# Half of the query tiles as fp16 pairs, top-k set up inside its generator, and 64 instead of 72 expert columns in the first stash

## The chip, the core and the metric

The kernel runs on one core of one Trainium2 chip. The metric is the device time of one execution in microseconds. The kernel before was measured three times: 982.04, 983.15 and 983.37 us, median 983.15 us. One execution was also profiled; its own time was 982.88 us, of which the profile's span (first to last instruction) is 980.8 us.

## What is computed

One decoder block on 256 tokens of width 1024: an attention mixer (nothing of it is touched here), and behind it a product-key expert layer (PEER), then a final RMSNorm. Of the expert layer, cut to what matters:

```python
def peer_ffn(h, wq, sub_keys, u, v):            # 16384 experts = 128 x 128, 8 heads, top 16
    ...
    q = (xc @ wq).reshape(PEER_CHUNK, PEER_HEADS, 2, PEER_QDIM // 2)   # 16 query tiles of 128
    sub = jnp.einsum('thpd,pkd->thpk', q, sub_keys)
    sv, si = lax.top_k(sub, PEER_TOPK)                                 # per head and half
    cand = sv[:, :, 0, :, None] + sv[:, :, 1, None, :]
    ...
    best, pos = lax.top_k(cand, PEER_TOPK)
    g = jax.nn.softmax(best, axis=-1)
    act = jax.nn.gelu(jnp.einsum('td,thkd->thk', xc, u[eid]))
    return jnp.einsum('thk,thkd->td', g * act, v[eid])
```

## The kernel before, in words

The kernel gathers no experts. It computes all 16384 activations as 128 columns j of 128 experts each (NJ = 128) and multiplies them by a gate matrix that is zero outside the chosen experts. Its stages behind the attention mixer are these.

**Inputs (u stage).** `u_step(j)` (L826) loads 512 KB of `peer_u` (`raw`, 5 buffers), splits the tile into two fp16 halves, and multiplies with the token matrix h, which is itself held as an fp16 pair `h16`: 8 blocks of the inner dimension times 3 products, 24 matmuls of 256 columns by `mm3` (L88). The split is `split16` (L800): ScalarE writes the high half (L805), VectorE the remainder with a checksum into `chk` (L806). The halves go to `w_hi` for even and `w_lo` for odd j, 3 buffers each. A GELU on ScalarE (L846) then writes column j of a stash, fp32, one slice of 256 tokens for each j. The stash has two tiles: `st0` with HJ = 72 columns and `st1` with the other 56; `st1` takes the memory of the top-k tiles and exists only once these are closed.

**Top-k beside it.** `topk_gen` (L868) is a generator whose pieces are pumped between the u steps (L1054). For each of 8 heads: two query tiles (`wq`, L872), two sets of sub-key scores with a top 16 on VectorE (`sub_scores`, L881), and a top 16 of 80 candidate sums. Query tiles 0 to 3 (heads 0 and 1) are made earlier; the other 12 are made here, each as 8 matmuls in fp32 over `wraw` (3 buffers) and the fp32 copy `h2`, which the profile lists as 16 instructions (L877). Then two groups of 14 pieces turn the winners into one-hot keys `kT` and gates `gT`. The pump schedule is none or one piece a step to j = 11, then 2, 2, 1 in turn to j = 29, then one a step; the 64 pieces end at j = 58.

**Gates.** `g_all(half)` (L1008) goes over 32 blocks of 8 tokens. `g_build` (L975) makes one-hot matrices A (128 columns) and B, Bl (as many columns as the stash half) on VectorE; `g_apply` (L994) makes 16 matmuls with that many columns each (L1000), and VectorE multiplies the result into the stash (L1004). Half 0 is paced over the u steps j = 62 to 123, 65 pieces. Columns j of the first stash that come after gating has begun (62 to 71) go another way: GELU into a tile `act` and a multiplication by the gates already there (L842 to L844).

**Outputs (v stage).** `v_step(j)` (L1091) loads 512 KB of `peer_v`, splits it in the same way, splits the stash column into `wt` (3 buffers, L1071 and L1076) and makes 12 matmuls of 512 columns (L1089). Half 1 of the gates is paced over the first HJ - 6 = 66 of these steps. From j = HJ on, `tail_prep` (L1118) loads 8 tiles of `ada_w` into the same `raw` buffers, one a step, and reduces them on VectorE (L1121). Small inputs of the tail are loaded by POOL's queue into `st0`, whose columns are free by then: `scratch(i)` (L1104) is its i-th stretch of four columns. `xc`, 1 MB, goes to stretches 16 and 17 (L1113).

**Repeated half.** Sums of the residues (`chk`) and of the first high halves (`big`) are tested at the end (`all_fit`, L1163). Only if one is out of range does a second program part (L1205) repeat the expert layer in another format; in these runs it is jumped over.

**Order.** The framework orders the instructions of each engine before the run, by priority (the place in the program) among those that its own model finds ready. `tc.high_priority(offset=None)` (L809, L873) puts loads and splits to the front of that order. At run time each engine works strictly in that order.

Of the kernel before, what the change touches and what calls it, by code (L numbers as in the profile page):

```python
# [13 lines left out]
F32 = mybir.dt.float32  # L14
# [43 lines left out]
def block_kernel(ctx: ExitStack, tc: tile.TileContext, I, out):  # L58
# [48 lines left out]

    SU, SH, SW, SV = 2.0 ** 13, 2.0 ** 8, 2.0 ** -3, 2.0 ** 9
    hchk = keep.tile([P, KD], F32, name="hchk")
    big = keep.tile([P, 3 + KD], F32, name="big")  # L110


    ph1 = ExitStack()
# [652 lines left out]
    for k in range(KD):  # L766
        t = nrm[:, k % 2]
        V.tensor_mul(t, x2g[:, k, 0:T], rstd2)
        S.activation(h2[:, k], t, AF.Identity, bias=mod[:, 24 + k:25 + k])
        S.activation(h16[0][:, k], t, AF.Identity, bias=shs[:, k:k + 1], scale=SH, accum_out=big[:, 3 + k:4 + k])  # L770
        V.scalar_tensor_tensor(h16[1][:, k], h2[:, k], SH, h16[0][:, k], ALU.mult, ALU.subtract,
                               accum_out=hchk[:, k:k + 1])
    qe = h2_pool.tile([P, 4, T], F32, name="qe")
# [6 lines left out]

    GS = 2.0 ** 15
    NJ = 128
    HJ = 72
    st0_pool = ctx.enter_context(tc.tile_pool(name="stash0", bufs=1))
    st = [st0_pool.tile([P, HJ, T], F32, name="st0")]
    NCHK = 3 * NJ + KD
    LOW = 2.0 ** 17
    LIM = 2.0 ** 16

# [2 lines left out]
    gT = keep2.tile([P, 2, T, 2], F16, name="gT")  # L792
    iota = keep2.tile([P, P], F16, name="iota")
    chk = keep2.tile([P, NCHK], F32, name="chk")
    G.memset(chk[:, 0:3 * NJ], 0.0)
    G.tensor_copy(chk[:, 3 * NJ:], hchk)
    first_one = {}
    bad_flag = keep2.tile([1, 1], I32, name="bad_flag")

    def split16(src, hi, lo, scale, i):  # L800
        kw = {}
        if i < 2 * NJ and i // NJ not in first_one:
            first_one[i // NJ] = i
            kw = dict(accum_out=big[:, 1 + i // NJ:2 + i // NJ])
        S.activation(hi, src, AF.Copy, scale=scale, **kw)  # L805
        V.scalar_tensor_tensor(lo, src, scale, hi, ALU.mult, ALU.subtract, accum_out=chk[:, i:i + 1])  # L806

    def load_split16(src, scale, i):
        with tc.high_priority(offset=None):  # L809
            t = load(src)  # L810
            hl = hl_pool.tile([P, D], F32R, name=("w_hi", "w_lo")[i % 2]).bitcast(F16)
            split16(t, hl[:, 0:D], hl[:, D:2 * D], scale, i)
        return hl[:, 0:D], hl[:, D:2 * D]
# [1 line left out]
    pg = ctx.enter_context(tc.tile_pool(name="pg", bufs=2, space=PSUM, reuse_waits="tile"))  # L815
    ps_u = ExitStack()
    pu = ps_u.enter_context(tc.tile_pool(name="pu", bufs=3, space=PSUM, reuse_waits="tile"))
    tk_stack = ExitStack()
    tk = tk_stack.enter_context(tc.tile_pool(name="tk", bufs=2, reuse_waits="tile"))
    tk1 = tk_stack.enter_context(tc.tile_pool(name="tk1", bufs=1, reuse_waits="tile"))  # L820

    act_box, hr_box = [], []
    done_j = [0]
    gated = [0]
# [20 lines left out]
        if n < T:  # L845
            S.activation(w[:, n:T], ps[:, n:T], AF.Gelu_apprx_tanh, scale=scale)  # L846

    iota_i = tk1.tile([P, P], I32, name="iota_i")
    G.iota(iota_i, pattern=[[1, P]], base=0, channel_multiplier=0)
    G.tensor_copy(iota, iota_i)  # L850
    c15 = tk1.tile([P, PH * TK], U32, name="c15")
    G.memset(c15, 15)
    sk = tk1.tile([P, 2, P], F32, name="sk")
    nc.scalar.dma_start(sk, I["peer_sub_keys"])
    nc.scalar.dma_start(h2d, h2)
    sv = tk1.tile([P, 2, 2, PH, TK], F32, name="sv")
    si = tk1.tile([P, 2, 2, PH, TK], U32, name="si")
    best = tk1.tile([P, 2, PH, TK], F32, name="best")
    bpos = tk1.tile([P, 2, PH, TK], U32, name="bpos")

    def top16(vals, tmp, vout, iout):
        V.max(vout[:, 0:8], vals)
        V.max_index(iout[:, 0:8], vout[:, 0:8], vals)
# [1 line left out]
        V.max(vout[:, 8:16], tmp)  # L865
        V.max_index(iout[:, 8:16], vout[:, 8:16], tmp)

    def topk_gen():  # L868
        for h in range(PH):
            qs = {p: qe[:, 2 * h + p] for p in range(2)} if h < 2 else {}  # L870

            def wq(p):  # L872
                with tc.high_priority(offset=None):  # L873
                    w = load(I["peer_wq"][2 * h + p], pool=tk, name="wraw", bufs=3)
                ps = pu.tile([P, T], F32, name="up")
                for k in range(KD):
                    PE.matmul(ps, w[:, k * P:(k + 1) * P], h2[:, k], start=k == 0, stop=k == KD - 1)  # L877
                qs[p] = tk.tile([P, T], F32, name="qT")
                S.copy(qs[p], ps)

            def sub_scores(p):  # L881
                sps = pg.tile([P, NT, P], F32, name="gps").rearrange("p a b -> p (a b)")[:, 0:256]
# [9 lines left out]
            for f, p in ((wq, 0), (wq, 1), (sub_scores, 0), (sub_scores, 1))[2 if h < 2 else 0:]:  # L892
# [144 lines left out]
    tg = topk_gen()  # L1037
    alive = True
    gg = None
    for j in range(NJ):  # L1040
        if not alive and gg is None:
            tk_stack.close()
            st1_pool = ctx.enter_context(tc.tile_pool(name="stash1", bufs=1))
            st.append(st1_pool.tile([P, NJ - HJ, T], F32, name="st1"))
            act_stack = ExitStack()
            act_box.append(act_stack.enter_context(tc.tile_pool(name="actp", bufs=2)))
            h2_stack.close()
            gp_stack = ExitStack()
            gp_box.append(gp_stack.enter_context(tc.tile_pool(name="gp", bufs=2, side="right", reuse_waits="tile")))
            gg, first = g_all(0), j + 3  # L1050
        u_step(j, True)
        done_j[0] = j + 1
        if alive:
            alive = pump(tg, j % 2 if j < 12 else (2, 2, 1)[j % 3] if j < 30 else 1)  # L1054
        elif j >= first:
            paced(gg, j - first, NJ - 4 - first)
    ps_u.close()
    act_stack.close()
    w_pool = ctx.enter_context(tc.tile_pool(name="wp", bufs=LAST))

    def outputs(half, gg):

        inner = ExitStack()
        py = inner.enter_context(tc.tile_pool(name="py", bufs=1, space=PSUM))
        if not half:
            wl_pool = inner.enter_context(tc.tile_pool(name="wl", bufs=LAST, side="right"))
# [43 lines left out]
        fg = scratch(1)  # L1110
        nc.gpsimd.dma_start(fg, I["final_g"].partition_broadcast(P))
        xf = [scratch(4), scratch(5)]
        xc = scratch(16, 2).rearrange("p (k t) -> p k t", k=KD)  # L1113
        nc.gpsimd.dma_start(xc, x2d)

        ada_b2 = scratch(15)[:, 0:48]
# [46 lines left out]
        def all_fit():  # L1163

            ok = scratch(2)[:, 0:NCHK]
            V.tensor_mul(ok, chk, chk)
            V.tensor_scalar(ok, ok, LIM * LIM, None, ALU.is_lt)
            V.tensor_mul(big[:, 1:], big[:, 1:], big[:, 1:])
            V.tensor_reduce(big[:, 0:1], ok, axis=AX.X, op=ALU.min)
            V.tensor_scalar_mul(big[:, 0:1], big[:, 0:1], LOW / (P - 0.5))  # L1170
            ps = pg.tile([P, NT, P], F32, name="gps").rearrange("p a b -> p (a b)")[0:1, 0:3 + KD]
            PE.matmul(ps, ones[:, 0:1], big, start=True, stop=True)
            small = scratch(2)[0:1, 0:3 + KD]
# [27 lines left out]

    outputs(True, g_all(1))
    gp_stack.close()
    rv = nc.values_load(bad_flag, min_val=0, max_val=1)
    with tc.If(rv > 0):  # L1205

        again = ExitStack()
        pu = again.enter_context(tc.tile_pool(name="pu", bufs=2, space=PSUM))
        gated[0] = 0
# [14 lines left out]
                pass  # L1224
        again.close()
        outputs(False, None)


def bucket_onehot():
# [67 lines left out]
```

## Time and profile before

| | us |
|---|---|
| median of 3 runs (982.04 to 983.37) | 983.15 |
| profiled execution, its own time | 982.88 |
| its span | 980.8 |
| TensorE (PE) busy in the span | 934.2 (95%) |
| VectorE (DVE) busy | 766.8 (78%) |
| ScalarE (ACT) busy | 494.2 (50%) |

How to read it: PE is TensorE's matmuls, PEld its weight loads, which overlap them; POOL is GpSimd, SP the engine that issues most DMAs. Matmuls are pipelined, each is listed longer (0.27 us for 256 columns) than the distance between two starts (0.11 us), so the distance of starts is what a matmul costs in a row of them. VectorE's rows overlap their successor by about 0.08 us in the same way. L12 is line 12 of the kernel before.

### The profile page before, as it was taken

What the parts mean: (1) busy time and instruction counts of PE and PEld (TensorE: products, weight loads), DVE (VectorE), ACT (ScalarE), POOL (GpSimd) and SP (SyncE); (2) the same over time, 40 slices, a digit from 0 to 9 for tenths busy, and PEclk for the clock granted to TensorE, in tenths of its full rate; (3) what the DMA queues carried; (4) which work ended last, traced back from release to release, by engine and by line L of the source; (5) the groups of instructions that cost most, each with busy time, mean ns of one, the idle gap of its engine ahead of it and who ended that gap; (6) DMA issues with size and microseconds to landing.
All of it is one profiled execution on the core that took longest, in us unless ns stands there. A gap on an engine that the chain in (4) does not pass through costs nothing.

```text
span 980.8 us, 18690 instructions
## 1 busy us (share of the span) xinstructions
PE 934.2 (95%) x7120; PEld 686.2 (70%) x7120; DVE 766.8 (78%) x2033; ACT 494.2 (50%) x899; POOL 17.9 (2%) x32
## 2 busy tenths in 40 slices
PE   5698997989999999999999999999999999999995
PEld 3697776979888888889999999544444443454442
DVE  6597879778657599658888888799999998656564
ACT  4246876475323365544444444544544554555542
POOL 0100010000000000000000000000000000000001
PEclk9899899899999999999999999999999999999998
DMA  8997646677554345765555555665555669756631
GB/s 285 319 329 252 218 130 211 224 252 263 174 193 151 108 166 179 248 203 177 190 175 191 175 187 179 204 205 193 184 189 188 214 208 332 235 178 207 199 124 48
DMA packets 54709, 198.26 MB, mean 202 GB/s; under 512 B 6269, under 2 KB 6605, under 8 KB 54226
## 3 DMA queue, kind: packets, MB, share of 16 engines
q1 hardware_dynamic: 52642, 189.90, 58.0%
q0 software_dynamic: 1248, 5.33, 2.1%
q10 hardware_dynamic: 720, 1.74, 0.5%
q8 instruction: 58, 0.95, 0.4%
q14 instruction: 41, 0.34, 0.1%
HBM read 193.22 MB, written 3.74 MB: 201 GB/s over the span
## 4 chain that ended last, share of the span: by engine, by line
PE 81%; DVE 7%; DMA 6%; ACT 3%; issue 2%; SPq 0%; DVEq 0%; ACTq 0%
PE y L1089 28%; PE up L89 11%; PE up L91 11%; PE up L90 11%; PE up L877 4%; PE gps L1000 3%; DMA raw<-in_ada_w_dram 3%; DMA adaw<-in_ada_w_dram 2%; PE mm L90 1%; PE mm L91 1%; PE mm L89 1%; PE lg L362 1%; PE o L536 1%; DVE w_lo L74 1%; PE gps L885 1%
## 5 line engine op out<-in xcount | busy, mean ns | idle before, releaser
L1089 PEld LDWEIGHTS <-wt 128*128 128x128 f16 x1500 | 143.9, 98 | 170.2 <-DVE wt L806 4.7
L805 ACT ACTIVATE w_lo<-raw 128x1024 f16<-128x1024 f32 x128 | 135.3, 1057 | 173.9 <-PE y L1089 83.3
L805 ACT ACTIVATE w_hi<-raw 128x1024 f16<-128x1024 f32 x128 | 135.2, 1056 | 170.5 <-PE up L91 85.4
L806 DVE SCALAR_TENSOR_TENSOR w_lo<-raw,w_lo 128x1024 f16<-128x1024 f32 x128 | 156.5, 1222 | 62.9 <-ACT w_lo L805 60.5
L806 DVE SCALAR_TENSOR_TENSOR w_hi<-raw,w_hi 128x1024 f16<-128x1024 f32 x128 | 156.2, 1220 | 54.6 <-ACT w_hi L805 54.4
L1089 PE MATMUL y<-w_hi,wt 128*128 128x512 f16 x756 | 174.0, 379 | 2.1 <-DVE wt L806 2.1
L1089 PE MATMUL y<-w_lo,wt 128*128 128x512 f16 x744 | 171.0, 379 | 0.2
L89 PE MATMUL up<-h,w_hi 128*128 128x256 f16 x512 | 139.6, 273 | 2.1 <-ACT bq L777 2.1
L90 PE MATMUL up<-h,w_hi 128*128 128x256 f16 x512 | 139.6, 273 | 0.0
L91 PE MATMUL up<-h,w_hi 128*128 128x256 f16 x512 | 139.6, 273 | 0.0
L89 PE MATMUL up<-h,w_lo 128*128 128x256 f16 x504 | 137.4, 273 | 0.0
L90 PE MATMUL up<-h,w_lo 128*128 128x256 f16 x504 | 137.4, 273 | 0.0
L91 PE MATMUL up<-h,w_lo 128*128 128x256 f16 x504 | 137.4, 273 | 0.0
L806 DVE SCALAR_TENSOR_TENSOR wt<-st,wt 128x256 f16<-128x256 f32 x128 | 53.7, 420 | 4.7 <-ACT wt L805 4.7
L90 PEld LDWEIGHTS <-w_hi 128*128 128x128 f16 x512 | 50.1, 98 | 8.2 <-issue 2.3
L805 ACT ACTIVATE wt<-st 128x256 f16<-128x256 f32 x128 | 51.3, 401 | 7.6 <-PE y L1089 5.6
L90 PEld LDWEIGHTS <-w_lo 128*128 128x128 f16 x512 | 50.1, 98 | 6.0
L91 PEld LDWEIGHTS <-w_lo 128*128 128x128 f16 x512 | 50.1, 98 | 5.8
L91 PEld LDWEIGHTS <-w_hi 128*128 128x128 f16 x512 | 50.1, 98 | 5.8
L89 PEld LDWEIGHTS <-w_lo 128*128 128x128 f16 x512 | 50.1, 98 | 5.7
L89 PEld LDWEIGHTS <-w_hi 128*128 128x128 f16 x512 | 50.2, 98 | 5.5
L984 DVE TENSOR_TENSOR B<-iota,kT 128x576 f16<-128x576 f16 (+1 forms) x64 | 27.2, 425 | 28.8 <-PE gps L1000 28.8
(370 smaller groups left out, 1505.8 us busy)
## 6 DMA issues: line engine op xcount, KB each, us to landing
raw<-in_peer_u_dram SPq DMA_DIRECT2D x128, 512.0 KB, 3.5
raw<-in_peer_v_dram SPq DMA_DIRECT2D x128, 512.0 KB, 4.2
adal<-in_ada_w_dram SPq DMA_DIRECT2D x24, 512.0 KB, 4.3
raw<-in_w_inK_dram SPq DMA_DIRECT2D x16, 512.0 KB, 8.3
adaw<-in_ada_w_dram SPq DMA_DIRECT2D x16, 512.0 KB, 8.6
wraw<-in_peer_wq_dram SPq DMA_DIRECT2D x12, 512.0 KB, 4.4
raw<-in_cmp_w_dram SPq DMA_DIRECT2D x8, 512.0 KB, 5.0
raw<-in_w_out_dram SPq DMA_DIRECT2D x8, 512.0 KB, 4.3
```

What stands on the lines that cost most here:

```text
L74: return (eng or V).tensor_sub(lo, src, hi.bitcast(F32))
L89: PE.matmul(ps, w[0], m[0], start=start, stop=False)
L90: PE.matmul(ps, w[0], m[1], start=False, stop=False)
L91: PE.matmul(ps, w[1], m[0], start=False, stop=stop)
L362: PE.matmul(out, q[x][pr, ts], rhs, start=i == 0, stop=i == 2)
L536: PE.matmul(o[:, h * 64:(h + 1) * 64], pt[:, h * P:(h + 1) * P], vst[sb][:, b, g], start=False, stop=bi == len(blocks) - 1 and h == 3)
L805: S.activation(hi, src, AF.Copy, scale=scale, **kw)
L806: V.scalar_tensor_tensor(lo, src, scale, hi, ALU.mult, ALU.subtract, accum_out=chk[:, i:i + 1])
L877: PE.matmul(ps, w[:, k * P:(k + 1) * P], h2[:, k], start=k == 0, stop=k == KD - 1)
L984: V.tensor_tensor(pairs(x), io, kT[:, i, t0:t0 + NT, None, :].to_broadcast(four), ALU.is_equal)
L1000: PE.matmul(ps[:, q, 0:n], A[:, q], Bg[i][:, q], start=i == 0, stop=i == 1)
L1089: PE.matmul(yps[t][n], w[:, ts], m[:, ns], start=j == 0 and first, stop=j == NJ - 1 and last)
```

## The change

1. Of each head from 2 to 7, the first query tile (p = 0, six of the twelve) goes through `load_split16` and `mm3`, as a u step does: split by ScalarE and VectorE into a `w_hi` buffer, 24 fp16 matmuls of 256 columns against `h16`, and a scaled copy. Its checksum goes to new columns of `chk`, its first high half to a new column of `big`. The second tile (p = 1) stays in fp32; its load is no longer inside `high_priority`.
2. The set-up of the top-k (pools, iota, the load of the sub-keys `sk`) moves into the generator as a first piece, pumped once ahead of the loop, behind the store `h2d`, so that the repeated half can run the whole top-k again.
3. The pump schedule: one piece a step from j = 12, two at every fourth step to j = 35 and at every sixth after that. The pieces end at j = 60.
4. HJ = 64: both stash halves and both gate passes have 64 columns. Half 0 is gated over j = 64 to 123 (60 steps), so that no column of the first stash takes the `act` way; half 1 over the first 58 v steps; `tail_prep` starts at j = 64.
5. `xc` goes to stretches 8 and 9 (columns 32 to 39) instead of 16 and 17 (columns 64 to 71).
6. `chk` grows from 392 to 408 columns, `big` from 11 to 12; pools are opened and closed in other places; the repeated half is longer.

```diff
-    HJ = 72
+    HJ = 64
...
-    NCHK = 3 * NJ + KD
+    NCHK = 3 * NJ + 2 * PH + KD
...
-    def load_split16(src, scale, i):
+    def load_split16(src, scale, i, **kw):
         with tc.high_priority(offset=None):
-            t = load(src)
+            t = load(src, **kw)
...
-    def topk_gen():
+    def topk_gen(pools, pu, h2, qe):
+        tk = pools.enter_context(tc.tile_pool(name="tk", bufs=2, reuse_waits="tile"))
...
+        nc.scalar.dma_start(sk, I["peer_sub_keys"])
...
+        yield
         for h in range(PH):
...
             def wq(p):
-                with tc.high_priority(offset=None):
-                    w = load(I["peer_wq"][2 * h + p], pool=tk, name="wraw", bufs=3)
-                ps = pu.tile([P, T], F32, name="up")
-                for k in range(KD):
-                    PE.matmul(ps, w[:, k * P:(k + 1) * P], h2[:, k], start=k == 0, stop=k == KD - 1)
+                i = 2 * h + p
                 qs[p] = tk.tile([P, T], F32, name="qT")
-                S.copy(qs[p], ps)
+                kw = dict(pool=tk, name="wraw", bufs=3)
+                if qe is not None and p == 0:
+                    hi, lo = load_split16(I["peer_wq"][i], SU, i - 2 * PH, **kw)
+                    ps = pu.tile([P, T], F32, name="up")
+                    for k in range(KD):
+                        c = slice(k * P, (k + 1) * P)
+                        mm3(ps, (hi[:, c], lo[:, c]), (h16[0][:, k], h16[1][:, k]), k == 0, k == KD - 1)
+                    S.activation(qs[p], ps, AF.Copy, scale=1.0 / (SU * SH))
+                else:
+                    w = load(I["peer_wq"][i], **kw)
+                    ps = pu.tile([P, T], F32, name="up")
+                    for k in range(KD):
+                        PE.matmul(ps, w[:, k * P:(k + 1) * P], h2[:, k], start=k == 0, stop=k == KD - 1)
+                    S.copy(qs[p], ps)
...
+    nc.scalar.dma_start(h2d, h2)
+    tk_stack = ExitStack()
+    tg = topk_gen(tk_stack, pu, h2, qe)
+    alive = pump(tg, 1)
...
-            alive = pump(tg, j % 2 if j < 12 else (2, 2, 1)[j % 3] if j < 30 else 1)
+            alive = pump(tg, j % 2 if j < 12 else 2 if j % (4 if j < 36 else 6) == 0 else 1)
...
-        xc = scratch(16, 2).rearrange("p (k t) -> p k t", k=KD)
+        xc = scratch(8, 2).rearrange("p (k t) -> p k t", k=KD)
```

## Rows read from the trace of the kernel before

**Rows 1.** The table of stages (busy time of each engine in stretches of the span): the twelve query tiles (250 to 342), the two groups of 14 pieces (342 to 400), the u steps with gates (430 to 618), the v steps with gates (to 780) and with the ada loads (to 834). Columns: stretch, its length, busy us and instructions of PE, PEld, DVE, ACT, POOL, granted clock (1.00 is 2.4 GHz), DMA share, GB/s.
```profile
250.00:342.00 92.00, 92.00 (x656) 81.90 (x654) 58.43 (x314) 31.26 (x60) 0.00 (x0) 1.00 0.46 155
342.00:400.00 58.00, 58.00 (x533) 51.95 (x531) 57.05 (x159) 32.61 (x51) 0.00 (x0) 1.00 0.53 173
430.00:618.00 188.00, 188.00 (x2083) 170.15 (x2081) 160.22 (x305) 88.09 (x144) 0.00 (x0) 1.00 0.56 184
618.00:780.00 162.00, 162.00 (x1133) 79.49 (x1131) 146.38 (x367) 79.70 (x117) 1.11 (x2) 1.00 0.61 197
780.00:834.00 54.00, 51.81 (x309) 23.82 (x306) 47.43 (x115) 26.02 (x39) 1.09 (x2) 1.00 0.76 265
```

**Rows 2.** The waits of PE's matmul queue from 205 us to the end, the two longest in total: who waited for whom, us, times, longest.
```profile
PE y L1089 <- DVE wt L806: 2.1, 3, 0.9
PE up L89 <- ACT bq L777: 2.1, 1, 2.1
```

**Rows 3.** The chain that ended last, in order of time, among the query tiles: start, us, what. L877 x32 is two fp32 query tiles, L885 x8 the scores of both.
```profile
252.34 6.91 PE up L877 x32
261.87 0.89 PE gps L885 x8
```

**Rows 4.** The timeline of ScalarE beside the u steps: the split of two successive `peer_u` tiles, each started when TensorE gives a buffer back, so that the starts are one u step apart.
```profile
370.00 1.06 ACT L805 ACTIVATE w_lo<-raw 128x1024 f16<-128x1024 f32 x1 [1.29 <-PE up L91]
...
372.62 1.06 ACT L805 ACTIVATE w_hi<-raw 128x1024 f16<-128x1024 f32 x1 [1.29 <-PE up L91]
```

**Rows 5.** The table of stretches again, one full cycle of the query tiles (three u steps, two fp32 tiles, their scores), the second of three such.
```profile
267.84:283.50 15.66, 15.66 (x115) 13.95 (x113) 10.62 (x59) 5.26 (x10) 0.00 (x0) 1.00 0.48 170
```

**Rows 6.** The timeline of VectorE: one split remainder and the row behind it, beginning where the split's own cost ends.
```profile
341.31 1.23 DVE L806 SCALAR_TENSOR_TENSOR w_hi<-raw,w_hi 128x1024 f16<-128x1024 f32 x1 [5.00 <-ACT w_hi L805]
342.45 0.08 DVE L806 DVE_READ_ACCUMULATOR w_hi<-raw,w_hi 128x1 f32 x1
```

**Rows 7.** The table of stretches in the two groups of 14 pieces and behind VectorE's part of them, 16 us each.
```profile
362.00:378.00 16.00, 16.00 (x149) 14.36 (x148) 15.97 (x37) 8.11 (x13) 0.00 (x0) 1.00 0.52 170
...
394.00:410.00 16.00, 16.00 (x149) 14.34 (x148) 10.19 (x18) 8.25 (x13) 0.00 (x0) 1.00 0.85 288
```

**Rows 8.** DMA issues of SP and ACT: of SP in order of time, among the query tiles and where loads of `ada_w` (not in `high_priority`) meet those of `peer_v` (in it); then, from the table of issues, KB each and median us to landing.
```profile
191.99 1.37 SPq L69 DMA_DIRECT2D wraw<-in_peer_wq_dram  x3
...
600.31 193.64 SPq L69 DMA_DIRECT2D raw<-in_peer_v_dram  x70
795.95 0.33 SPq L69 DMA_DIRECT2D raw<-in_ada_w_dram  x1
798.64 0.33 SPq L69 DMA_DIRECT2D raw<-in_peer_v_dram  x1
...
wraw<-in_peer_wq_dram SPq DMA_DIRECT2D x12, 512.0 KB, 4.4
...
h2d<-h ACTq DMA_DIRECT2D x1, 1024.0 KB, 10.3
```

**Rows 9.** The sub-keys and the store `h2d` on ACT's queue (start, length of the issue), and the first use of the sub-keys by TensorE: duration min/median/max, first and last start.
```profile
200.83 0.34 ACTq L854 DMA_DIRECT2D sk<-in_peer_sub_keys_dram  x1
...
216.32 0.34 ACTq L855 DMA_DIRECT2D h2d<-h  x1
...
L885 PE MATMUL gps<-sk,qe x16: 275/275/276, 221.6 to 244.2; 128*128 128x128 f32 x16
```

**Rows 10.** The chain that ended last in both gated stages: the 16 gate matmuls of a block with 72 columns (u stage) and with 56 (v stage), and two v steps between two blocks.
```profile
565.98 0.52 PE gps L1000 x16
...
641.96 0.41 PE gps L1000 x16
642.37 5.18 PE y L1089 x24
```

**Rows 11.** The timeline of VectorE in the v stage: the start of one period of two steps and one gate block, a `wt` remainder in it, and the start of the next. A wait stands in brackets.
```profile
642.38 0.39 DVE L984 TENSOR_TENSOR B<-iota,kT 128x448 f16<-128x448 f16 x1 [0.31 <-PE gps L1000]
...
645.27 0.42 DVE L806 SCALAR_TENSOR_TENSOR wt<-st,wt 128x256 f16<-128x256 f32 x1
...
647.97 0.39 DVE L984 TENSOR_TENSOR B<-iota,kT 128x448 f16<-128x448 f16 x1 [0.31 <-PE gps L1000]
```

**Rows 12.** The same operations of both gate passes with other sizes (448 = 8 tokens x 56 columns, 576 = 8 x 72): count, busy us, mean ns, from the groups by form.
```profile
L1004 DVE TENSOR_TENSOR st<-gps,st 128x576 f32<-128x576 f32 x29 | 21.8, 751 | 0.0
L1004 DVE TENSOR_TENSOR st<-gps,st 128x448 f32<-128x448 f32 x32 | 19.8, 618 | 0.0
L991 DVE TENSOR_TENSOR B<-B,gT 128x576 f16<-128x576 f16 x32 | 14.6, 458 | 1.1
L991 DVE TENSOR_TENSOR B<-B,gT 128x448 f16<-128x448 f16 x32 | 12.4, 388 | 0.0
```

**Rows 13.** Where `xc` and the ada loads meet: POOL's issue of `xc`, the chain's DMA piece (an ada load, issue to landing), and the three waits of TensorE.
```profile
815.64 0.54 POOL L1114 DMA_DIRECT2D st<-x2d  x1 [32.89 <-DVE wt L806]
...
815.03 7.49 DMA raw<-in_ada_w_dram
...
819.17 1.90 PE L1089 MATMUL y<-w_hi,wt 128*128 128x512 f16 x8 [0.78 <-DVE wt L806]
...
825.44 1.90 PE L1089 MATMUL y<-w_hi,wt 128*128 128x512 f16 x8 [0.92 <-DVE wt L806]
...
831.46 1.90 PE L1089 MATMUL y<-w_hi,wt 128*128 128x512 f16 x8 [0.42 <-DVE wt L806]
```

More of the change, by code (lines that the diff above doesn't have):

```diff
@@ L109, in block_kernel @@
     hchk = keep.tile([P, KD], F32, name="hchk")
-    big = keep.tile([P, 3 + KD], F32, name="big")
+    big = keep.tile([P, 4 + KD], F32, name="big")
     ph1 = ExitStack()
@@ L769, in block_kernel @@
         S.activation(h2[:, k], t, AF.Identity, bias=mod[:, 24 + k:25 + k])
-        S.activation(h16[0][:, k], t, AF.Identity, bias=shs[:, k:k + 1], scale=SH, accum_out=big[:, 3 + k:4 + k])
+        S.activation(h16[0][:, k], t, AF.Identity, bias=shs[:, k:k + 1], scale=SH, accum_out=big[:, 4 + k:5 + k])
         V.scalar_tensor_tensor(h16[1][:, k], h2[:, k], SH, h16[0][:, k], ALU.mult, ALU.subtract,
@@ L794, in block_kernel @@
     chk = keep2.tile([P, NCHK], F32, name="chk")
-    G.memset(chk[:, 0:3 * NJ], 0.0)
-    G.tensor_copy(chk[:, 3 * NJ:], hchk)
+    G.memset(chk[:, 0:NCHK - KD], 0.0)
+    G.tensor_copy(chk[:, NCHK - KD:], hchk)
     first_one = {}
@@ L801, in split16 @@
         kw = {}
-        if i < 2 * NJ and i // NJ not in first_one:
-            first_one[i // NJ] = i
-            kw = dict(accum_out=big[:, 1 + i // NJ:2 + i // NJ])
+        kind = 2 if i < 0 else i // NJ
+        if i < 2 * NJ and kind not in first_one:
+            first_one[kind] = i
+            kw = dict(accum_out=big[:, 1 + kind:2 + kind])
+        if i < 0:
+            i += NCHK - KD
         S.activation(hi, src, AF.Copy, scale=scale, **kw)
         V.scalar_tensor_tensor(lo, src, scale, hi, ALU.mult, ALU.subtract, accum_out=chk[:, i:i + 1])
-    def load_split16(src, scale, i):
+    def load_split16(src, scale, i, **kw):
         with tc.high_priority(offset=None):
-            t = load(src)
+            t = load(src, **kw)
             hl = hl_pool.tile([P, D], F32R, name=("w_hi", "w_lo")[i % 2]).bitcast(F16)
@@ L817, in block_kernel @@
     pu = ps_u.enter_context(tc.tile_pool(name="pu", bufs=3, space=PSUM, reuse_waits="tile"))
-    tk_stack = ExitStack()
-    tk = tk_stack.enter_context(tc.tile_pool(name="tk", bufs=2, reuse_waits="tile"))
-    tk1 = tk_stack.enter_context(tc.tile_pool(name="tk1", bufs=1, reuse_waits="tile"))
     act_box, hr_box = [], []
@@ L846, in u_step @@
             S.activation(w[:, n:T], ps[:, n:T], AF.Gelu_apprx_tanh, scale=scale)
[L848 to L859, printed above, removed]
     def top16(vals, tmp, vout, iout):
@@ L866, in top16 @@
         V.max_index(iout[:, 8:16], vout[:, 8:16], tmp)
-    def topk_gen():
+    def topk_gen(pools, pu, h2, qe):
+        tk = pools.enter_context(tc.tile_pool(name="tk", bufs=2, reuse_waits="tile"))
+        tk1 = pools.enter_context(tc.tile_pool(name="tk1", bufs=1, reuse_waits="tile"))
+        iota_i = tk1.tile([P, P], I32, name="iota_i")
+        G.iota(iota_i, pattern=[[1, P]], base=0, channel_multiplier=0)
+        G.tensor_copy(iota, iota_i)
+        c15 = tk1.tile([P, PH * TK], U32, name="c15")
+        G.memset(c15, 15)
+        sk = tk1.tile([P, 2, P], F32, name="sk")
+        nc.scalar.dma_start(sk, I["peer_sub_keys"])
+        sv = tk1.tile([P, 2, 2, PH, TK], F32, name="sv")
+        si = tk1.tile([P, 2, 2, PH, TK], U32, name="si")
+        best = tk1.tile([P, 2, PH, TK], F32, name="best")
+        bpos = tk1.tile([P, 2, PH, TK], U32, name="bpos")
+        yield
@@ L869, in topk_gen @@
         for h in range(PH):
-            qs = {p: qe[:, 2 * h + p] for p in range(2)} if h < 2 else {}
+            qs = {p: qe[:, 2 * h + p] for p in range(2)} if qe is not None and h < 2 else {}
             def wq(p):
-                with tc.high_priority(offset=None):
-                    w = load(I["peer_wq"][2 * h + p], pool=tk, name="wraw", bufs=3)
-                ps = pu.tile([P, T], F32, name="up")
-                for k in range(KD):
-                    PE.matmul(ps, w[:, k * P:(k + 1) * P], h2[:, k], start=k == 0, stop=k == KD - 1)
-                qs[p] = tk.tile([P, T], F32, name="qT")
-                S.copy(qs[p], ps)
+                i = 2 * h + p
+                qs[p] = tk.tile([P, T], F32, name="qT")
+                kw = dict(pool=tk, name="wraw", bufs=3)
[12 more added lines that the diff above has]
+                    S.copy(qs[p], ps)
@@ L890, in sub_scores @@
                     top16(sub[:, t], tmp, sv[:, t, p, h], si[:, t, p, h])
-            for f, p in ((wq, 0), (wq, 1), (sub_scores, 0), (sub_scores, 1))[2 if h < 2 else 0:]:
+            for f, p in ((wq, 0), (wq, 1), (sub_scores, 0), (sub_scores, 1))[2 if qs else 0:]:
                 f(p)
@@ L1035, in pump @@
         return True
-    tg = topk_gen()
-    alive = True
+    nc.scalar.dma_start(h2d, h2)
+    tk_stack = ExitStack()
+    tg = topk_gen(tk_stack, pu, h2, qe)
+    alive = pump(tg, 1)
+    late = ctx.enter_context(ExitStack())
     gg = None
@@ L1042, in block_kernel @@
             tk_stack.close()
-            st1_pool = ctx.enter_context(tc.tile_pool(name="stash1", bufs=1))
+            st1_pool = late.enter_context(tc.tile_pool(name="stash1", bufs=1))
             st.append(st1_pool.tile([P, NJ - HJ, T], F32, name="st1"))
@@ L1058, in block_kernel @@
     act_stack.close()
-    w_pool = ctx.enter_context(tc.tile_pool(name="wp", bufs=LAST))
     def outputs(half, gg):
         inner = ExitStack()
+        w_pool = inner.enter_context(tc.tile_pool(name="wp", bufs=LAST))
         py = inner.enter_context(tc.tile_pool(name="py", bufs=1, space=PSUM))
@@ L1170, in all_fit @@
             V.tensor_scalar_mul(big[:, 0:1], big[:, 0:1], LOW / (P - 0.5))
-            ps = pg.tile([P, NT, P], F32, name="gps").rearrange("p a b -> p (a b)")[0:1, 0:3 + KD]
+            ps = pg.tile([P, NT, P], F32, name="gps").rearrange("p a b -> p (a b)")[0:1, 0:4 + KD]
             PE.matmul(ps, ones[:, 0:1], big, start=True, stop=True)
-            small = scratch(2)[0:1, 0:3 + KD]
+            small = scratch(2)[0:1, 0:4 + KD]
             V.tensor_scalar(small, ps, LOW, None, ALU.is_lt)
@@ L1203, in block_kernel @@
     gp_stack.close()
+    late.close()
     rv = nc.values_load(bad_flag, min_val=0, max_val=1)
     with tc.If(rv > 0):
+        again = ExitStack()
+        pu = again.enter_context(tc.tile_pool(name="pu", bufs=2, space=PSUM))
+        h2 = again.enter_context(tc.tile_pool(name="h2p", bufs=1, side="right")).tile([P, KD, T], F32, name="h2")
+        nc.sync.dma_start(h2, h2d)
+        for _ in topk_gen(again, pu, h2, None):
+            pass
+        again.close()
+        late = ExitStack()
+        st[1] = late.enter_context(tc.tile_pool(name="stash1", bufs=1)).tile([P, NJ - HJ, T], F32, name="st1")
         again = ExitStack()
@@ L1226, in block_kernel @@
         outputs(False, None)
+        late.close()
 def bucket_onehot():
```

## The prediction

> **What bounds the kernel now.** I read the table of stages first, then TensorE's waits, then the chain. In every stage behind attention TensorE is busy for the whole stretch at a granted clock of 1.00, save 2.2 us of the 54 us in which the ada loads run [rows 1]. Matmul rows overlap one another, so full busy time alone would prove little; the waits settle it: from 205 us to the end the matmul queue waits 2.1 us for ScalarE's `bq` ahead of the first u step and 2.1 us for `wt` in the ada stretch, and nothing else above 0.2 us [rows 2]. So from 216 to 962 us the time is the number of matmuls times their distance. What shortens TensorE's queue shortens the kernel by as much, if the other engines still keep ahead. VectorE is the one to watch: 58 of 92 us among the query tiles, 57 of 58 in the groups of 14 pieces, 146 of 162 beside the v steps [rows 1].
>
> **The query tiles.** Two fp32 tiles take 6.91 us of the chain, one 3.455 us [rows 3]. A u step, which has the 24 fp16 matmuls that a pair tile will have, takes 2.62 us (372.62 - 370.00) [rows 4]. Three steps, two tiles and their scores give 3 x 2.62 + 6.91 + 0.89 = 15.66 us, the measured cycle [rows 3, 5], so the two prices hold. Six tiles change: 6 x (3.455 - 2.62) = **-5.0 us**. All of it lies on TensorE's queue.
>
> What is added lies on ScalarE and VectorE: per pair tile one split of each. On VectorE that costs 1.14 us (341.31 to 342.45) [rows 6]. In the new schedule a head takes four u steps instead of three: 4 x 2.62 + 3.455 + 2.62 + 0.89 = 17.4 us of TensorE, against 10.62 us of VectorE now plus two more splits, 12.9 us [rows 5]: 74%, so TensorE covers it. ScalarE has 5.26 us there now and gains two splits of 1.06 us [rows 4, 5]. Cost zero. `w_hi` serves three tiles in four steps, with three buffers: a tile can be split a whole cycle ahead. If that cover went, each pair tile could wait for its split, 1.06 + 1.14 us, 13 us for six.
>
> The second tile's load leaves the front of the order. Nothing in the trace shows this load so; the nearest rows are the ada loads, also outside, which take their turn among hurried `peer_v` loads although 58 of these 128 are still to come [rows 8]. Buffers are handed out in program order, and SP is idle between. I take zero; the worst is a landing of 4.4 us for each of six, 26 us [rows 8].
>
> **The groups of 14 pieces** now get 24 steps instead of 28, 62.9 us. VectorE was saturated there for 32 us and more while TensorE lost nothing, because splits go first; from 394 us on it has room again, though the 28 steps from 342 us run to 415 [rows 1, 7]. The transposes that wait for it come two steps earlier, but the last head's scores also end a step earlier before the group begins. I take zero; the bound is those two steps once, 5.2 us.
>
> **The set-up.** The load of the sub-keys now stands behind `h2d` on ACT's queue. It is issued at 200.8 us and used at 221.6; `h2d` waits for the last of h until 216.3 [rows 9]. The planner takes what is ready, so I expect the sub-keys ahead of it still: zero. Behind it, they might come as late as 216.3 + 10.3 = 226.6 us, a wait of 5 us [rows 8, 9].
>
> **64 and 64 columns.** A gate block's 16 matmuls take 0.52 us with 72 columns and 0.41 with 56 [rows 10]; halfway, 0.465. 32 x 0.52 + 32 x 0.41 = 29.8 us before, 64 x 0.465 = 29.8 us after: zero. The `act` way that goes is ScalarE and VectorE work off the path: zero. The Trainium skill speaks against the straight line here: its page "TensorE: Matmul & The Clock Gate", section "Back-to-back issue gap", gives every matmul of 1 to 64 moving columns about 60 cycles. By it 64 columns would cost as 56 do, and the sum would be 3.5 us lower; the trace's 0.41 / 16 = 25.8 ns at 56 columns is about 62 cycles of 2.4 GHz, already above that.
>
> **VectorE beside the v steps** is the doubtful part. A period is 5.59 us, two steps and a block (647.97 - 642.38), with one wait of 0.31 us [rows 11]; at 90% busy it holds 5.05 us of work [rows 1]. The four splits in it take 2 x 1.14 + 2 x 0.35 = 2.98 us [rows 6, 11], the block 2.07. Eight columns more add half of the step from 56 to 72: 0.035 us to each of three operations, 0.067 to the stash product, 0.17 in all [rows 12]. And the 65 pieces must now fit 58 steps, not 66. Work: 29 x 2.98 + 32 x 2.24 = 158 us. TensorE: 58 x 2.59 + 32 x 0.465 = 165 us [rows 10]. So 96% instead of 89%, and in seven steps two pieces meet. In such a step VectorE owes 1.49 + 2.24 = 3.73 us while TensorE takes 2.59 + 0.465 = 3.06; it makes that up at (5.645 - 5.22) / 2 = 0.2 us a step, in three or four steps of the eight to the next. Three `wt` buffers ahead carry 0.7 us. I take zero; the other end is a rival.
>
> **`xc` moves.** It is 1 MB, issued at 815.6 us among the eight ada loads; an ada load issued just before takes 7.5 us to land where the usual is under 5, VectorE waits for it in order, `wt` comes late, and TensorE waits 0.78, 0.92 and 0.42 us [rows 13]. In columns 32 to 39 it is free some 30 steps earlier, where DMA is about 60% busy [rows 1]. The first wait is of ada loads issued before `xc`; the other two (1.34 us) I count as its own: **-1.3 us**, between 0 and -2.1. What is late next is the same wait, from the ada loads alone.
>
> **The tail.** Three checksum operations over 408 columns instead of 392, no row of them above 0.6 us: +0.05 us. The longer repeated half is jumped over: zero.
>
> **Sum.** -5.0 - 1.3 + 0.05 = -6.3 us on the profiled execution's own 982.88 us: 976.6. The median of the runs shown is 0.27 us above that execution, so **976.9 us**.
>
> **Rivals.**
> - **VectorE falls behind beside the v steps, and the kernel is slower** (14%). Place: the seven double steps, some 612 to 780 us. It decides once `wt`, which is not hurried, is queued behind the gate pieces and hurried splits, so that its three buffers run out: then each double step costs at least the 0.7 us owed and at most a full gate block of 2.24 us, 5 to 16 us together. For it: 96%, and `wt` is already what TensorE waits for when it waits. Against: a real wait of 0.31 us per period today, and no wait of TensorE in 162 us. From 8 us on the kernel is slower: 976.9 + 9 = 986 us.
> - **Part of the gain is lost** (13%): single waits of 2 to 5 us for the two-steps-earlier transposes, the sub-keys or a few `wt`; 979 to 982 us, say 980.5.
> - **The loads outside the front come late** (4%): 976.9 + up to 26 us, 990 to 1003.
> - **More is gained** (6%): 64 columns cost what 56 do, 32 x 0.11 = 3.5 us, and all 2.1 us of waits go: 976.9 - 3.5 - 0.8 = 972.6 us. The first half of it is what the page named above would have.
> - **It does not do what it says** (1%): the new checks call the repeated half, and the expert layer runs twice, some 700 us more.
>
> **How the numbers follow.** The forecast has 60%, with 975.5 to 978.5 as its own range (`xc` between its bounds, a microsecond for another order of instructions); 2% are for what I have not seen. The range for eight in ten runs from 975 us to 984 us: it leaves out the large gain, the late loads, the repeat and the upper part of the first rival. About 0.2%, 2 us, is what a measurement of this kernel can tell from no change. Faster than 981.2: the forecast, the large gain and half of the partial loss, 0.73. Within: the rest of that and the mild first rival, 0.11. Slower: 0.16.
>
> **What would show it.** Among the query tiles: 24 fp16 matmuls in place of 16 fp32 ones for every second tile, 2.62 us on the chain, and TensorE without a wait. Gate blocks of 0.465 us in both passes. `xc` issued before 760 us and TensorE's wait for `wt` in the ada stretch under 1 us. If VectorE is the trouble, TensorE's wait for `wt` between 610 and 780 us grows from nothing to several us, in about seven places. I am wrong if TensorE waits for `wraw` or `w_hi` among the query tiles, or if the sub-keys are issued behind `h2d`.

## The result: 975.35 us, and where the time went

The kernel after takes **975.35 us** (median of 4 runs, 974.87 to 975.86), the kernel before 982.6 us (4 runs); the ratio is 0.9923, 95% interval 0.991 to 0.9935. The forecast was 976.9 us, with 975 to 984 us for eight runs in ten: the result lies near the lower end of that range, and 0.15 us below the forecast's own 975.5 to 978.5. The profiled execution of the kernel after took 974.93 us, its span is 973.2 us.

A span is cut best where TensorE passes from one kind of work to the next. The timelines of TensorE give three such starts: the first u step, the first v step, and the first of the last three v steps, which run in an order of their own. The kernel before:

```profile
216.33 0.27 PE L89 MATMUL up<-h,w_hi 128*128 128x256 f16 x1 [2.06 <-ACT bq L777]
...
617.66 0.59 PE L1089 MATMUL y<-w_hi,wt 128*128 128x512 f16 x2
...
961.30 0.81 PE L1161 MATMUL y<-w_lo,wt 128*128 128x512 f16 x3
```

The same starts in the kernel after:

```profile
216.59 0.27 PE L89 MATMUL up<-h,w_hi 128*128 128x256 f16 x1 [2.06 <-ACT bq L777]
...
611.29 1.03 PE L1103 MATMUL y<-w_hi,wt 128*128 128x512 f16 x4
...
954.22 0.81 PE L1175 MATMUL y<-w_lo,wt 128*128 128x512 f16 x3
```

| us | before | after | difference | forecast |
|---|---|---|---|---|
| up to the first u step | 216.33 | 216.59 | +0.26 | 0 |
| u stage | 401.33 | 394.70 | -6.63 | -5.0 - 1.76 |
| v stage | 343.64 | 342.93 | -0.71 | +1.76 - 1.3 |
| tail | 19.50 | 18.98 | -0.52 | +0.05 |
| span | 980.8 | 973.2 | -7.6 | -6.3 |

(1.76 is 32 gate blocks at 0.055 us less in the u stage, and again 32 at 0.055 us more in the v stage; the forecast set one against the other.) The u stage came as forecast. The v stage gave 1.2 us more. The first and the last line vary from one execution to the next: over the profiles of this case the first u step starts between 214.6 and 217.7 us (218.8 in one kernel with a longer wait there), and the tail takes 18.1 to 19.7 us. The two middle lines are the ones to compare. Of these the u stage is the steadier one: it takes 394.70 or 394.71 us in five profiles of kernels with the same instructions there, while the v stages of the four kernels that share the v stage of the kernel after take 342.55 to 342.93 us, so that a difference of some 0.4 us in the v stage means nothing.

The table of stages of the kernel after, in the stretches of [rows 1]:

```profile
250.00:342.00 92.00, 92.00 (x766) 82.24 (x765) 68.05 (x324) 40.34 (x69) 0.00 (x0) 1.00 0.51 167
342.00:400.00 58.00, 58.00 (x517) 51.82 (x515) 53.53 (x159) 34.08 (x53) 0.00 (x0) 1.00 0.54 169
430.00:618.00 188.00, 188.00 (x2070) 167.07 (x2068) 155.57 (x302) 88.98 (x137) 0.00 (x0) 1.00 0.58 186
618.00:780.00 162.00, 162.00 (x1195) 81.61 (x1194) 154.91 (x383) 78.09 (x115) 1.91 (x4) 1.00 0.61 198
780.00:834.00 54.00, 53.44 (x256) 25.46 (x254) 42.93 (x107) 28.49 (x47) 0.28 (x1) 1.00 0.81 274
```

TensorE is busy throughout at a clock of 1.00, save 0.6 us of the ada stretch. VectorE rose to 68 us among the tiles (58 before) and to 154.9 of 162 us beside the v steps, 96%, as counted. (The stages have moved: the query tiles now last to about 355 us and the groups of 14 pieces to about 418, so the second stretch no longer holds the groups alone.) The two longest waits of TensorE's matmul queue in total (from 205 us, as in [rows 2]) and the chain:

```profile
PE up L89 <- ACT bq L777: 2.1, 1, 2.1
PE y L1103 <- DVE wt L810: 0.6, 1, 0.6
```

```profile
290.12 3.46 PE up L890 x16
307.57 3.46 PE up L890 x16
...
600.04 0.93 PE gps L1012 x32
...
633.58 2.59 PE y L1103 x12
636.63 5.18 PE y L1103 x24
642.28 5.18 PE y L1103 x24
```

One fp32 tile (L890) per cycle of 307.57 - 290.12 = 17.45 us; 32 gate matmuls of 64 columns in 0.93 us, 0.465 a block; and a double step of the v stage at 633.58, 2.59 + 0.465 = 3.05 us, without a wait behind it.

Most of the 1.2 us lies in the ada stretch. TensorE's timeline there, before (with the three rows of [rows 13] that carry waits between these) and after:

```profile
817.36 1.03 PE L1089 MATMUL y<-w_hi,wt 128*128 128x512 f16 x4
...
820.90 2.75 PE L1089 MATMUL y<-w_lo,wt 128*128 128x512 f16 x12
823.49 1.03 PE L1089 MATMUL y<-w_hi,wt 128*128 128x512 f16 x4
...
827.17 3.00 PE L1089 MATMUL y<-w_lo,wt 128*128 128x512 f16 x12
830.01 1.03 PE L1089 MATMUL y<-w_hi,wt 128*128 128x512 f16 x4
...
833.20 3.03 PE L1089 MATMUL y<-w_lo,wt 128*128 128x512 f16 x12
836.06 2.11 PE L1089 MATMUL y<-w_hi,wt 128*128 128x512 f16 x9
```

```profile
791.99 1.03 PE L1103 MATMUL y<-w_hi,wt 128*128 128x512 f16 x4
793.57 1.90 PE L1103 MATMUL y<-w_hi,wt 128*128 128x512 f16 x8 [0.56 <-DVE wt L810]
795.31 2.75 PE L1103 MATMUL y<-w_lo,wt 128*128 128x512 f16 x12
```

A v step is 2.59 us from start to start. Before, five steps are longer: 3.54, 3.68 and 3.19 us with a listed wait, 2.84 and 2.86 without one: 3.2 us lost, where the view of waits shows 2.1. After, one step takes 3.32 us: 0.7 lost. The difference is 2.4 us, not 1.3. `xc` is issued at 719.33 us, as foretold before 760, and the one wait left is under 1 us. A wait is listed some 0.17 us short because the row of the matmul before it is listed that much longer than its distance, and a wait shorter than that shows only as a longer step.

### The profile page after: what moved, and what is told of

Its sections match the earlier page's. It is cut to its first block, busy times and chain, and to the rows that moved or that the text cites. A ratio compares the mean times of both kernels' runs of the same rounds, so it can differ in the third digit from the quotient of the medians.

```text
span 973.2 us, 18795 instructions
## 1 busy us (share of the span) xinstructions
PE 929.2 (95%) x7168; PEld 683.1 (70%) x7168; DVE 769.5 (79%) x2039; ACT 502.0 (52%) x899; POOL 17.9 (2%) x32
## 4 chain that ended last, share of the span: by engine, by line
PE 85%; DVE 6%; ACT 4%; DMA 3%; issue 1%; SPq 0%; ACTq 0%; DVEq 0%
PE y L1103 31%; PE up L89 12%; PE up L90 12%; PE up L91 12%; PE gps L1012 3%; PE up L890 2%; DMA adaw<-in_ada_w_dram 2%; PE mm L90 1%; PE mm L91 1%; PE mm L89 1%; PE lg L362 1%; PE o L536 1%; DVE w_lo L74 1%; PE gps L897 1%; DVE adal L151 1%
## 5 line engine op out<-in xcount | busy, mean ns | idle before, releaser
L89 PE MATMUL up<-h,w_hi 128*128 128x256 f16 x560 | 152.7, 273 | 2.1 <-ACT bq L777 2.1
L91 PE MATMUL up<-h,w_hi 128*128 128x256 f16 x560 | 152.7, 273 | 0.0
L90 PE MATMUL up<-h,w_hi 128*128 128x256 f16 x560 | 152.7, 273 | 0.0
L90 PEld LDWEIGHTS <-w_hi 128*128 128x128 f16 x560 | 54.8, 98 | 8.5 <-issue 2.3
L91 PEld LDWEIGHTS <-w_hi 128*128 128x128 f16 x560 | 54.8, 98 | 6.3
L89 PEld LDWEIGHTS <-w_hi 128*128 128x128 f16 x560 | 54.8, 98 | 6.0
L846 ACT ACTIVATE st<-up 128x256 f32<-128x256 f32 x127 | 46.5, 367 | 0.0
```

The source lines that it names most:

```text
L89: PE.matmul(ps, w[0], m[0], start=start, stop=False)
L90: PE.matmul(ps, w[0], m[1], start=False, stop=False)
L91: PE.matmul(ps, w[1], m[0], start=False, stop=stop)
```

## The experiments

Each was run beside the kernel before on the same chip, whose medians were 983.4 to 983.8 us there; ratios are to it. Stage times are those of the profiled execution, cut as above; the time of the whole kernel is a median of several. A load is called hurried when it stands inside `high_priority`.

**All tiles in fp32 again.**

```diff
-                if qe is not None and p == 0:
+                if False:
```

(and one line that fills the unused column of `big`)

> The kernel after, with all twelve query tiles in fp32 again; everything else as after. Theory (six times the difference of 3.455 and 2.62 us, nothing hidden): 975.35 + 5.0 = 980.35 us, two tiles at 6.91 us on the chain, no new wait. Rival (the gain came from the other order of the pieces and of the set-up, or the splits cost TensorE something that is saved here): between 975.4 and 979 us.

Measured: 982.85 us, ratio 0.9989 (0.9979 to 0.9999); more than the theory gave, and the rival was on the other side. The u stage took 401.37 us, 6.7 more than after. This edit also took the first tile's load out of the hurried ones, so that none of the twelve was. TensorE's wait and the table of stretches at the start of the u stage:

```profile
PE up L89 <- ACT bq L777: 4.1, 1, 4.1
```

```profile
216.00:219.00 3.00, 0.23 (x3) 0.20 (x3) 3.00 (x10) 2.97 (x7) 0.00 (x0) 1.00 0.80 261
219.00:222.60 3.60, 3.60 (x21) 2.52 (x19) 1.66 (x5) 1.70 (x6) 0.19 (x1) 0.53 0.93 315
```

The wait for `bq` is 2 us longer, and behind it TensorE ran a u step at a granted clock of 0.53 in the mean of that stretch, almost all of it at the lower of its two levels (1.2 GHz), matmuls 0.21 us apart instead of 0.11: 1.7 us. So the next run left the load hurried.

**All tiles in fp32, the first load of each head hurried.** The branch for `p == 0` loads `wraw` in `high_priority` and makes the fp32 matmuls.

> The kernel after, with all twelve query tiles in fp32 and the first tile's load of each head still hurried, as it is in the kernel after; only the arithmetic of six tiles differs. Theory (in the run before this one the 3.4 us beyond the six tiles came from the load that was not hurried: TensorE waited longer for the last of attention and then ran a u step at half clock): the first u step starts near 216.6 us at full clock, the u stage takes 394.7 + 5.0 = 399.7 us, 980.35 us in all. Rival (the pair tiles' splits themselves order the start better): the first u step starts near 218.8 us, 402 us, 983 us in all.

Measured: 981.17 us, ratio 0.997 (0.9957 to 0.9983); u stage 399.70 us, 5.00 more than after, first u step at 215.69 us, wait for `bq` 2.1 us. For the u stage the theory held to the last digit. The whole time is 0.8 us above it, and the profiled execution, 978.41 us, was the shortest of the seven.

**All tiles as pairs.**

```diff
-                if qe is not None and p == 0:
+                if qe is not None:
```

> The kernel after, with the second query tile of each head as an fp16 pair too, split into w_lo buffers: all twelve tiles as pairs. Theory (TensorE's queue alone sets the time, and VectorE at some 14 us of work in a cycle of 16.6 us keeps ahead): 975.35 - 5.0 = 970.35 us, cycles of 16.6 us. Rival (the splits of six more tiles compete with those of the u steps, TensorE waits for w_hi or w_lo, at most 1.06 + 1.14 us for each of six): up to 13 us of that back, so anything from 972 to 983 us, with waits for VectorE among the query tiles.

Measured: **968.47 us**, ratio 0.9844 (0.9826 to 0.9863), faster than both kernels and 1.9 us below the theory. The u stage is 389.69 us, 5.01 less than after; the v stage 342.55 and the tail 18.16 account for another 1.2 us, both within their usual spread. One cycle in the table of stretches (VectorE is the third busy time):

```profile
288.60:305.21 16.61, 16.61 (x154) 14.99 (x153) 14.29 (x65) 8.50 (x15) 0.00 (x0) 1.00 0.58 192
```

VectorE has 14.3 us of work in 16.6 us and TensorE waits for nothing among the tiles.

**The kernel before with the pair tiles alone.** Columns, pump, `xc` and hurried loads as before; `load_split16` and `mm3` for `p == 0`.

> The kernel before, with the pair tiles alone: six query tiles split into w_hi buffers and multiplied in fp16; columns (72 and 56), the pump schedule, the place of xc and the hurried loads as before. Theory (the six tiles are worth their difference anywhere): u stage 401.33 - 5.0 = 396.3 us, the v stage as before with its three waits, 343.6 us, so 5.0 us less than the kernel before: 977.6 to 978.4 us. Rival (with three steps a head instead of four, w_hi's buffers or VectorE run short, at most 1.06 + 1.14 us for each of six tiles): u stage between 397 and 409 us, with waits for w_hi.

Measured: 979.28 us, ratio 0.9959 (0.9943 to 0.9974); u stage 396.33 us, 5.00 less than before, v stage 343.88 us with three waits for `wt`. The whole time is 0.9 us over the theory's range, the u stage as it said. Three times, from three sides, six tiles are worth 5.0 us. The three waits also show that the pair tiles have no part in the gain of the v stage.

**The kernel before with the early `xc` alone.**

```diff
-        xc = scratch(16, 2).rearrange("p (k t) -> p k t", k=KD)
+        xc = scratch(8, 2).rearrange("p (k t) -> p k t", k=KD)
```

> The kernel before, with one edit of the change alone: xc in columns 32 to 39 instead of 64 to 71. Theory (xc alone makes the losses of the ada stretch): 982.6 - 2.4 = 980.2 us or a little less, with at most one wait for wt there. First rival (as forecast): 981.3 us, the first of the three waits staying. Second rival (the waits hang on the ada loads and the gate pieces, not on xc): 982.6 us, three waits as before.

Measured: 982.17 us, ratio 0.9988 (0.9978 to 0.9998); v stage 341.26 us, 2.4 less than before, one wait of 0.47 us:

```profile
820.05 1.90 PE L1089 MATMUL y<-w_hi,wt 128*128 128x512 f16 x8 [0.47 <-DVE wt L806]
```

The stage gives the 2.4 us of the theory, with the first wait staying as in the first rival. The whole time does not bear it out to the full: its interval allows 0.2 to 2.2 us, and beginning and tail vary by as much. The 2.4 us thus rest on the stage, which with the late `xc` took 343.64 and 343.88 us in two kernels.

**The kernel after with the late `xc`.** A first version put the load's instruction ahead of the steps that read columns 64 to 71, so that those eight steps multiplied by `xc` instead of their gated activations. The run took 974.02 us, ratio 0.9903 (0.9885 to 0.992), v stage 343.15 us. The load went out at 776.87 us, in a gap of 7 us between two ada loads (774.34 and 781.34), and landed within 5.0 us, about when VectorE came to the first of the eight reductions, at 781.58 us. So this isn't the meeting that was to be tested; there `xc` lay near the ada loads while nobody awaited one of them, and the v stage shows no cost of it beyond its spread.

> The kernel after, with xc put into columns 64 to 71 again, so that its load is issued among the ada loads as before. Theory (the early xc is worth more than forecast, because every step of the ada stretch that lost time lost it through xc): TensorE's starts lose about 3.2 us in the ada stretch instead of 0.7, so 975.35 + 2.4 = 977.8 us, with several waits for wt in the profile. First rival (the term as forecast, 1.3 us, the rest being chance): 976.6 us. Second rival (the waits went because gates and ada loads meet otherwise with 64 columns, and xc has no part in it): 975.4 us and one wait as now.

The second version:

```diff
-        xc = scratch(8, 2).rearrange("p (k t) -> p k t", k=KD)
-        nc.gpsimd.dma_start(xc, x2d)
+        xc = st[1][:, 0:8]
...
             v_step(j)
+            if half and j == HJ + 7:
+                nc.gpsimd.dma_start(xc, x2d)
```

> The kernel after, with xc in columns 64 to 71 again and its load placed behind the step that reads the last of them, so that it is issued among the ada loads as in the kernel before. Theory (each lost step of the ada stretch lost its time through xc): the time from the first to the last v step grows from 342.93 by 2.4 to 345.3 us, 977.8 us in all, with several waits for wt. Rival (64 columns and gates that end before the ada loads have removed the waits): 342.9 and 975.4 us, one wait for wt as now.

Measured: 974.71 us, ratio 0.9912 (0.9898 to 0.9927); v stage 343.30 us, one wait of 0.9 us. The theory fell. The v stage is 0.4 us longer than in the kernel after, and this is not the late `xc`: it lies in the one wait, 18 us before `xc` is issued. No cost of the late `xc` shows. The timelines of TensorE (the wait), POOL and SP (issue of `xc`, issue of the last ada load) say why:

```profile
795.09 1.90 PE L1103 MATMUL y<-w_hi,wt 128*128 128x512 f16 x8 [0.94 <-DVE wt L810]
```

```profile
813.25 0.54 POOL L1165 DMA_DIRECT2D st<-x2d  x1 [31.82 <-DMA raw<-in_peer_v_dram]
```

```profile
799.19 0.33 SPq L69 DMA_DIRECT2D raw<-in_ada_w_dram  x1
```

With `HJ` at 64 the ada loads start at step 64 and are over by 799 us; 813 us is behind them. In the kernel before they went out from 795.95 us on [rows 8], with `xc` at 815.64 in their midst [rows 13].

**The late `xc` with the ada loads at every second step** (a second `yield` behind each of them):

> The late xc as in the run with it in columns 64 to 71, with the ada loads at every second v step instead of every step. Theory (the waits come from 1 MB of xc on top of a 512 KB ada load and a 512 KB peer_v load per step): with half the ada loads beside it the v stage loses under 1 us, 342.3 to 343.2 us in all, as with the early xc. Rival (xc alone disturbs the loads, or the ada reductions on VectorE wait for it in any case): the v stage stays over 344.5 us.

Measured: 980.02 us, ratio 0.9966 (0.9951 to 0.9981); v stage 348.04 us, 4.7 more than with the late `xc` alone. The theory's number missed by 5 us, and its premise, that the late `xc` alone would cost something, fell with the run before; but the transfers that it named do meet in the timelines. The spreading stretched the ada loads until `xc` met the last one (POOL, SP, VectorE, TensorE):

```profile
810.96 0.54 POOL L1166 DMA_DIRECT2D st<-x2d  x1 [30.88 <-PE y L1103]
```

```profile
813.28 0.33 SPq L69 DMA_DIRECT2D raw<-in_ada_w_dram  x1
```

```profile
819.95 1.23 DVE L1136 CUSTOM_DVE_ANT_0 raw<-raw,st 128x1024 f32<-128x1024 f32 x1 [3.71 <-DMA raw<-in_ada_w_dram]
```

```profile
822.93 3.34 PE L1103 MATMUL y<-w_hi,wt 128*128 128x512 f16 x8 [2.78 <-DVE wt L810]
```

That ada load landed 6.5 us after its issue; VectorE stood still for it for 3.7 us, the `peer_v` and `wt` splits stood behind it, and TensorE waited 2.8 us and then ran 8 matmuls in 3.34 us instead of 1.90, mostly at half clock (table of stretches):

```profile
822.90:824.60 1.70, 1.67 (x4) 0.59 (x5) 1.70 (x8) 0.00 (x0) 0.00 (x0) 0.50 0.85 292
```

An ada load that VectorE awaits while `xc` is on its way beside it: that is the mechanism that these rows and [rows 13] show. The ada loads spread with the early `xc` were not run; but of 5.9 us that the steps of this stretch lose, 0.7 lie ahead of the issue of `xc` and 5.1 behind it, 1.4 of them through the clock. Spreading does not help in itself; VectorE then waits for six of the eight loads, 0.4 to 3.7 us each, where it waits for one in the kernel after.

**The second gate pass over 48 and over 40 v steps.**

```diff
-                paced(gg, j, HJ - 6)
+                paced(gg, j, HJ - 16)
```

> The kernel after, with the second gate pass over 48 v steps instead of 58: 17 steps with two pieces instead of seven. Theory (VectorE's load is what the forecast counted, 96% in 58 steps): work 24 x 2.98 + 32 x 2.24 = 143 us against TensorE's 48 x 2.59 + 32 x 0.465 = 139 us, so TensorE now waits for wt in the gated steps, 2 to 6 us in all: 977 to 981 us. Rival (VectorE has more room than counted, or pieces can slip behind the 48 steps without anybody waiting): 975.4 us and no wait there.

> The kernel after, with the second gate pass over 40 v steps instead of 58: 25 steps with two pieces. Theory (once VectorE's work is above TensorE's, the difference is lost, save what the buffers carry): work 20 x 2.98 + 32 x 2.24 = 131.3 us against 40 x 2.59 + 32 x 0.465 = 118.5 us, 12.8 us; of the 4.0 us counted for 48 steps 2.6 were lost, so 11.4 us more than the kernel after: 986.7 us, with a v stage of 354 us. Rival (each double step costs a fixed sum, 2.6 us over 17 of them): 25 x 0.15 = 3.8 us, 979.2 us, a v stage of 346.8 us.

(`HJ - 24` in the second.) Measured: 977.6 us, ratio 0.9946 (0.9931 to 0.996), v stage 345.50; and 984.42 us, ratio 1.0008 (0.9994 to 1.0021), v stage 353.34, that is 2.6 and 10.4 us more than the 342.93 of the kernel after. The counted excess of VectorE's work over TensorE's was 4.0 and 12.8 us: 1.4 and 2.4 us are carried. The whole time with 40 steps is 2.3 us below the theory's 986.7. The fixed price of a double step (3.8 us for 25) is refuted. The waits are not all where the forecast put them; with 48 steps there is a single one, ahead of a gate block close to the end of the pass, and `wt` is not late at all:

```profile
752.42 0.20 PE L1012 MATMUL gps<-B,A 128*128 128x64 f16 x1 [2.68 <-DVE B L1003]
```

With 40 steps the two longest in total are these:

```profile
PE gps L1012 <- DVE B L1003: 4.8, 9, 1.4
PE y L1103 <- DVE wt L810: 2.8, 4, 1.1
```

The profiled execution of the second run (984.27 us) holds 1.7 us for a u step at half clock (last section).

## Why the prediction was right, and the term that was off

The forecast was 1.55 us too high. One term was mis-sized, `xc`; the others came as worked out, as far as the stages can tell.

**Query tiles, -5.0 us: right.** 5.00, 5.01 and 5.00 us in three pairs of kernels. The cover held too: VectorE did 13.06 us of work in a cycle of 17.45 us, where 12.9 in 17.4 had been counted, and had room for six more tiles.

**64 and 64 columns, zero: right, each half as worked out.** The block takes 0.465 us in both passes; the u stage with pairs went from 396.33 to 394.70, 1.63 us less for 1.76 counted, and the v stage with the early `xc` from 341.26 to 342.93, 1.67 more. The rule of the Trainium skill's page "TensorE: Matmul & The Clock Gate", section "Back-to-back issue gap", under which 64 columns would have cost as 56 do, did not hold: 0.465 / 16 = 29.1 ns at 64 columns is 70 cycles at 2.4 GHz, against 62 at 56.

**VectorE beside the v steps, zero: right.** 96% forecast, 96% measured, no wait behind the seven double steps. The margin was real but thin: ten steps fewer cost 2.6 us, eighteen fewer 10.4. The rival had a true mechanism and a wrong point: in these three kernels the loss begins where VectorE's whole work exceeds TensorE's, not where single steps owe some.

**`xc`, -1.3 us: the term that was mis-sized.** It measured 2.4 us in the kernel before alone (343.64 to 341.26) and 2.4 us in the lost steps from before to after. Both lie outside the bounds that it was given, 0 to 2.1 us. Its main fault was that it was read from the listed waits: the second and third are listed with 1.34 us, but the steps behind the first lose 2.2. The first wait was put down to ada loads issued ahead of `xc`, and that was right in the main: without `xc` there its step still loses 0.6 us of 0.95.

What the forecast didn't see at all is that the change removes this collision twice. Eight columns fewer start the ada loads eight steps sooner, which by itself takes them out of the way of the late `xc` (and VectorE comes to their reductions from 782.7 us on, with the first load issued at 769.8: it waits for one of eight, before for seven). So in the kernel after nothing measurable is left for the early `xc`: the move is worth 2.4 us alone, and none beside the smaller stash. The forecast gave the gain to the move alone. The collision that it named is real, but here the smaller stash, to which it gave nothing, would have removed it without the move; that the sign came out right for the reason given is in that part luck.

**Groups of 14 pieces, sub-keys, loads: zero, right.** In the kernel after the groups run from about 355 to 418 us; VectorE is busy for 57 of these 63 us and TensorE waits for nothing (table of stretches):

```profile
355.00:418.00 63.00, 63.00 (x579) 56.35 (x577) 57.05 (x144) 38.48 (x59) 0.00 (x0) 1.00 0.62 199
```

The sub-keys are issued at 201.09 us and `h2d` at 216.74, as before. The second tiles' loads outside the front cost nothing as they stand. That this is no law is shown by the run in which the first tiles' loads left it as well: the start of the u stage was then ordered in another way (a `wraw` load goes out at 205.54 us between `peer_u` loads, and ScalarE waits 1.2 us for one of these), and the wait for `bq` is 2 us longer, with the half clock behind it.

**The tail, +0.05: not measurable** under a spread of 1.6 us.

The rest of the distance, 976.9 to 975.35 us, is 1.0 us of the u and v stages together (7.3 us less, forecast 6.3), in the main the `xc` term; the last half microsecond is within the variation of beginning and tail.

## What to carry to other kernels

When one engine's queue sets the time, count its instructions by their distance and trust the sum, and compare two kernels stage by stage between starts of that queue: six tiles were worth 5.00 us to the last digit there, while whole times of one kernel differ by 3 us and more. Read lost time from the lengths of repeated steps, not from listed waits alone. And where a big transfer meets a series of loads that an engine awaits in order, look for every edit that shifts either of them in time: here the smaller stash moved the loads, so the gain of moving the transfer was made twice and counts once.

## What had not been expected of the hardware

TensorE's granted clock can fall behind a wait of a few us, and the same wait does not always do it. After the wait of some 2.06 us for `bq` it stayed at 1.00 in the profiles of before and after and in eight others. In the run with 40 gate steps, the same wait of the same length was followed by 16 matmuls at half clock (table of stretches):

```profile
214.60:216.00 1.40, 1.40 (x12) 1.16 (x12) 1.18 (x3) 1.40 (x3) 0.00 (x0) 0.85 0.64 181
216.00:218.60 2.60, 2.60 (x14) 1.80 (x13) 0.78 (x2) 0.35 (x2) 0.00 (x0) 0.50 0.88 202
```

Nine distances of 0.11 us, then sixteen of 0.21: its u stage is 396.37 us where the kernel after has 394.70. A wait of 2.68 us ahead of a gate block left the clock at 1.00 (48 steps), one of 2.78 us was followed by half clock (ada loads spread), and so was the one of 4.1 us (all tiles in fp32). So in these profiles a short wait costs its own length or 1.4 to 1.7 us more, and which of the two can differ between kernels with the same instructions up to there; what decides it was not settled here.
